# Cross-attention output by block of tokens for its last two column groups, and a hand-ordered second norm

## The chip, the cores and the metric

The kernel runs on one core of a Trainium2 chip. The metric is the time of one execution on the device in microseconds (us). Before the change it is 1125.58 us, the median of three runs (1125.52 to 1125.97).

The core's engines work side by side and each takes its instructions in order: TensorE (PE in the profile; PEld is its weight load), VectorE (DVE), ScalarE (ACT), GpSimd (POOL) and SyncE (SP), which issues the loads from memory.

## The reference

One layer of an encoder on 256 tokens of 2048 columns, all in float32. Around the change it does this:

```python
x  = layer_norm(ALPHA * x + mix, ln1_g, ln1_b)
xa = memory_cross_attention(x, mem_n, w_q_mem, w_kv_mem, w_o_mem)   # ends with o @ w_o_mem, 512 x 2048
x  = layer_norm(ALPHA * x + xa, ln2_g, ln2_b)
ff = square(relu(x @ w_mlp_in)) @ w_mlp_out                          # 2048 x 8192 and back
x  = layer_norm(ALPHA * x + ff, ln3_g, ln3_b)
```

`layer_norm` subtracts the mean over a token's 2048 columns, divides by the standard deviation, multiplies by a gain and adds a bias.

## The kernel before, in words

**Numbers as pairs.** TensorE multiplies a rounded form of float32. Every operand is therefore kept as two parts: hi, which is the value rounded, and lo, which is the value less hi. A product is the sum of three: hi times hi, hi times lo, lo times hi. `split` (L77) makes the pair: ACT writes hi (L79), DVE subtracts for lo (L80).

**Tokens and tiles.** The 256 tokens are two blocks of 128. `res[b]` holds the residual of block b, tokens on partitions, 2048 columns. For the next matrix product the activations must be transposed: `x2t` holds 16 row tiles k of 128 columns, each with 256 tokens of hi and 256 of lo.

**Weights.** A `Stream` (L115) loads a weight unit (128 x 2048, one megabyte) into one of three raw tiles through SP and splits it in two halves of 1024 columns into `w_hi` and `w_lo`, of which there are four buffers each. A half's buffer comes free when the products that read it are done. `next()` gives one half.

**The cross-attention output** (L677 to L685). Four column groups n of 512; each takes two halves of `w_om`. `proj_tokens` (L150) makes 4 row tiles x 2 blocks x 3 products of 512 columns, block after block within a row tile; for n = 3 it goes by block: all of block 0, then block 1 in two halves of 256 columns. After each group DVE adds the PSUM tile to the scaled residual (L683) and takes the statistics of that piece (L490).

**The second norm** (L689, `norm_transposed`, L501). `moments` gives mean and 1/deviation of a block: aggregate on DVE (L495), a small addition on DVE (L88), a power of -1/2 on POOL (L91). `scale(n)` subtracts the mean and multiplies, in place, on 512 columns of each block (L513, DVE). `turn(k)` treats two row tiles: four transposes on PE into one PSUM tile (L526; there are four such tiles), gain and bias into a temporary, the first row tile on ACT (L534), the second on DVE (L531), then one split of both row tiles into `x2t` (L79, L80). The norm is cut into pieces, scale 0, turn 0, scale 1, turn 2 and so on. Between them four halves of the first MLP weights are split (L692); four others already lie in `wide_0`.

**The first MLP products** (L721). `together` makes four column tiles at once, row tile by row tile: for each of 16 row tiles four pairs of a 512-column product (L193) and a 256-column product (L195; L192 for the last row tile). Two row tiles of `x2t` and one half of weights serve each step. Later column tiles take their weights from `s_in`.

**What sets the order.** A scheduler places each engine's instructions by a timing reckoning of its own and by priority in the order of the program. `pin` (L74) puts an instruction behind whatever the program had last for the same engine. Before the change only the splits of those four halves of MLP weights are pinned here; a hand-made edge keeps the later scalings behind the first.

Of the kernel before, what the change touches and what calls it, by code (L numbers as in the profile page):

```python
# [11 lines left out]
F32 = mybir.dt.float32  # L12
F32R = mybir.dt.float32r
BF16 = mybir.dt.bfloat16
AF = mybir.ActivationFunctionType
# [23 lines left out]
def encoder_kernel(ctx: ExitStack, tc: tile.TileContext, t, out):  # L39
# [56 lines left out]
    def pump(n=1):  # L96
        """Issues n of the pieces of work that run beside the products."""
        for _ in range(n):
            if side:
                side.popleft()()  # L100
# [4 lines left out]
    def busy(n):  # L105
        """Keeps the array's clock up while it waits."""
        ps = acc_tile()
        for _ in range(n):
            tc.keep_in_program_order(
                nc.tensor.matmul(ps, ones, ones[:, None, :].broadcast_to([P, 4, P]),  # L110
                                 start=True, stop=True))
# [3 lines left out]
    class Stream:  # L115
        """Halves of weight units, loaded and split in the order in which they are asked for."""

# [30 lines left out]

    # xt: [128, k, 512] holds the transposed activations, hi in 0:256, lo in 256:512.
    def proj_tokens(stream, xt, nk, cols, before=None, by_block=None, wide=None):  # L150
        """Tokens on partitions: two PSUM tiles [128, cols], one a block of tokens. By block,
        the second comes in two halves of the columns, each behind the one before."""
        ps = [acc_tile() for _ in range(NB + bool(by_block))]
# [29 lines left out]
    def cols_mm(ps, hi, lo, xt, k, nk):  # L183
        """Columns on partitions: PSUM [128, 256] += a [k, 128] tile of weights."""
        nc.tensor.matmul(ps, hi, xt[:, k, 0:S], start=k == 0, stop=False)  # L185
        nc.tensor.matmul(ps, hi, xt[:, k, S:2 * S], start=False, stop=False)  # L186
        nc.tensor.matmul(ps, lo, xt[:, k, 0:S], start=False, stop=k == nk - 1)  # L187

    def cols_mm_wide(ps, hi, lo, xt, k, nk):
        """The same into [128, 512]: the products with the activations' lo in 256:512."""  # L190
        if k == nk - 1:
            nc.tensor.matmul(ps[:, 0:S], lo, xt[:, k, 0:S], start=False, stop=False)  # L192
        nc.tensor.matmul(ps, hi, xt[:, k, :], start=k == 0, stop=k == nk - 1)  # L193
        if k < nk - 1:
            nc.tensor.matmul(ps[:, 0:S], lo, xt[:, k, 0:S], start=False, stop=False)  # L195

    def transpose_split(dst, src, k0, b, nk=4, width=P):
        """Transposes src [128 tokens, nk * 128] into dst[:, k0:k0+nk] at the block's place."""
        ps = att_tile()
        for j in range(nk):  # L200
            nc.tensor.transpose(ps[:, j * P:(j + 1) * P], src[:, j * P:(j + 1) * P], ident)
        o = b * P
        v = ps[:, :nk * P].rearrange("p (k c) -> p k c", c=P)
        split(dst[:, k0:k0 + nk, o:o + P], dst[:, k0:k0 + nk, S + o:S + o + P], v)

# [1 line left out]
    tab_a = resp.tile([P, D], F32, tag="res", name="tab_a")  # L207
# [7 lines left out]

# [1 line left out]
    xt_t = big.tile([P, KT * 512], F32R, tag="big", name="xt")  # L217
# [3 lines left out]
    def load_x(k):  # L221
        """The row tiles of x^T from k on."""
        n = 1 if k < 2 else 0 if k % 2 else 2
# [29 lines left out]

# [1 line left out]
    def latent(stream, g, dst):  # L255
# [11 lines left out]
    def qk_heads(ps, b, nh, tc_, ts_, dst, h0, sc=1.0):  # L267
        """RMS norm, gain and rotation of nh heads [128, nh * 128], then their transposes."""
        w = nh * DH
# [23 lines left out]

# [1 line left out]
    class Heads:  # L295
        """Heads of attention under way: the scores of one, the weights of the one before, the
        values of the one before that."""

# [15 lines left out]
    def softmax(terms, pt=None):  # L314
        """terms: (q [128, 512], k [128, 512]) pairs, hi | lo, summed into the scores.
        Returns the transposed weights of attention, hi | lo."""
        s = att_tile()
# [166 lines left out]

# [1 line left out]
    def stats_tile():  # L486
        return [small.tile([P, 5, 6], F32, tag="bn", name="bn"), 0]

    def stats(st, x):
        nc.vector.bn_stats(st[0][:, st[1], :], x)  # L490
        st[1] += 1

    def moments(st):
# [6 lines left out]

    def norm_transposed(x, sts, i, dst, vec=False, before=None):  # L501
        """x(b, n) <- (x(b, n) - mean) * rstd in place; dst <- its transpose with gain and bias, split.
        Returns the pieces of that work behind the moments."""
        mom = [moments(sts[b]) for b in range(NB)]

        ahead = []

        def scale(n):
            if before is not None:
                before(n)  # L510
            for b in range(NB):
                mu, r = mom[b]
                ins = nc.vector.tensor_scalar(out=x(b, n), in0=x(b, n), scalar1=mu, scalar2=r,  # L513
                                              op0=ALU.subtract, op1=ALU.mult)
                if n and ahead:
                    tc.add_manual_dep(ins.ins, ahead[0], mybir.DependencyInfo(
                        mybir.DependencyClass.NoSync, mybir.DependencyReason.DATA))
            if vec and not n:
                ahead.append(ins.ins.name)

        def turn(k, n=2):
            ps, y = att_tile(), tmp_tile()
            for j in range(n):
# [5 lines left out]
                g, c = gbt[:, i, 0, k + j:k + j + 1], gbt[:, i, 1, k + j:k + j + 1]  # L529
                if j == 1 and vec:  # L530
                    nc.vector.tensor_scalar(out=y[:, o], in0=ps[:, o], scalar1=g, scalar2=c,  # L531
                                            op0=ALU.mult, op1=ALU.add)
                else:
                    nc.scalar.activation(y[:, o], ps[:, o], AF.Identity, scale=g, bias=c)  # L534
            ins = split(dst[:, k:k + n, 0:S], dst[:, k:k + n, S:2 * S],
                        y[:, :n * S].rearrange("p (j c) -> p j c", j=n))

# [8 lines left out]
    def residual(name):  # L546
        """res <- res * gain + bias, as pieces."""
        rows = {}
# [22 lines left out]

# [1 line left out]
    sts = [stats_tile() for _ in range(NB)]  # L573
# [42 lines left out]

# [1 line left out]
    attC = big.tile([P, 8192], F32R, tag="big", name="attC")  # L618
# [4 lines left out]
    def together(nexts, xt_, mm, outs):  # L623
        """Several column tiles at once, k by k."""
        n = len(outs)
# [49 lines left out]
    pump(len(side))  # L675

    sts = [stats_tile() for _ in range(NB)]  # L677
    s_om = Stream(t["w_om"])
    for n in range(4):
        ps = proj_tokens(s_om, om, HM, 512, by_block=n == 3)  # L680
        for b, c, w, p_ in ps:
            r = res[b][:, n * 512 + c:n * 512 + c + w]
            nc.vector.scalar_tensor_tensor(out=r, in0=r, scalar=ALPHA, in1=p_[:, :w],  # L683
                                           op0=ALU.mult, op1=ALU.add)
            stats(sts[b], r)  # L685
    x2t = big3("x2t")
    s_mi0.pinned = True
    w_mi0 = [(wide_0[:, u, 0, :], wide_0[:, u, 1, :]) for u in range(4)]
    for i, piece in enumerate(norm_transposed(res_chunk, sts, 2, x2t, vec=True)):  # L689
        piece()  # L690
        if i in (5, 7, 9, 11):
            w_mi0.append(s_mi0.next())  # L692

# [1 line left out]
    s_in, s_mo = Stream(t["w_mi"]), Stream(t["w_mo"])  # L695
# [10 lines left out]
    def last_weights(k):  # L706
        """The last group's weights stay on chip whole, for one block of tokens after the other."""
        hi, lo = wide_w[0][:, k * 512:(k + 2) * 512], wide_w[1][:, k * 512:(k + 2) * 512]
# [65 lines left out]
def _rows(w, kt, cols):  # L774
    """[K, N] -> units [n * kgroups, 128, kt * cols]: kt row tiles of one group of columns."""
    k, n = w.shape
# [4 lines left out]
def _pairs(w, d):  # L781
    """Rotation pairs of each d columns side by side -> firsts, then seconds."""
    s = w.shape[:-1]
# [102 lines left out]
```

## Time and profile before

| | |
|---|---|
| median of the runs | 1125.58 us |
| profiled execution, span from first to last instruction | 1123.8 us |
| TensorE busy | 1108.1 us, 99% |
| DVE busy | 740.9 us, 66% |
| ACT busy | 541.4 us, 48% |
| last product of the cross-attention output ends | 393.97 us |
| first MLP product starts | 402.16 us |

Times within the execution are microseconds from the start of the span. A row of a time line gives start, duration, engine, line, operation, what is written from what, and how many instructions are merged in it; in brackets stands how long the engine sat idle before it and what ended that. A row of busy times by stretch gives the stretch, then the busy time of PE, PEld, DVE, ACT and POOL (with the number of instructions), then the granted share of TensorE's clock, the share of the DMA engines, and GB/s. A row of the chain of waits gives start, duration and what. Matmuls are pipelined: a product recorded with 0.39 us starts 0.23 us after the one before.

### The profile page before, as it was taken

What the parts mean: (1) busy time and instruction counts of PE and PEld (TensorE: products, weight loads), DVE (VectorE), ACT (ScalarE), POOL (GpSimd) and SP (SyncE); (2) the same over time, 40 slices, a digit from 0 to 9 for tenths busy, and PEclk for the clock granted to TensorE, in tenths of its full rate; (3) what the DMA queues carried; (4) which work ended last, traced back from release to release, by engine and by line L of the source; (5) the groups of instructions that cost most, each with busy time, mean ns of one, the idle gap of its engine ahead of it and who ended that gap; (6) DMA issues with size and microseconds to landing.
All of it is one profiled execution on the core that took longest, in us unless ns stands there. A gap on an engine that the chain in (4) does not pass through costs nothing.

```text
span 1123.8 us, 14990 instructions
## 1 busy us (share of the span) xinstructions
PE 1108.1 (99%) x6004; PEld 955.1 (85%) x6004; DVE 740.9 (66%) x1036; ACT 541.4 (48%) x778; POOL 38.2 (3%) x45
## 2 busy tenths in 40 slices
PE   9999999999999999999999999999999999999996
PEld 6988899888998878888888888888888888888885
DVE  5878677688798778855556664556665546665575
ACT  6555665546576355443345443344444334444440
POOL 1402000000100000000000000000000000000000
PEclk9999999999999999999999999999999999999998
DMA  9664454476466426655555555555555555555572
GB/s 336 223 225 151 150 187 150 152 241 243 161 225 252 150 75 225 226 187 187 187 190 189 185 186 192 201 199 188 184 186 198 188 188 187 188 187 187 190 260 76
DMA packets 37942, 215.85 MB, mean 192 GB/s; under 512 B 4336, under 2 KB 5232, under 8 KB 14192
## 3 DMA queue, kind: packets, MB, share of 16 engines
q1 hardware_dynamic: 37872, 214.89, 54.4%
q8 instruction: 47, 0.77, 0.3%
q14 instruction: 23, 0.19, 0.0%
HBM read 212.78 MB, written 2.10 MB: 191 GB/s over the span
## 4 chain that ended last, share of the span: by engine, by line
PE 96%; DMA 2%; DVE 1%; ACT 0%; issue 0%; SPq 0%; POOL 0%; DVEq 0%; ACTq 0%
PE acc L193 21%; PE acc L147 17%; PE acc L145 17%; PE acc L146 17%; PE acc L195 10%; PE acc L187 2%; PE acc L186 2%; PE acc L185 2%; PE att L526 1%; DMA raw<-in_w_qa 1%; PE att L341 1%; DMA raw<-in_w_ka 1%; PE acc L192 1%; PE att L147 1%; PE att L146 1%; PE att L145 1%
## 5 line engine op out<-in xcount | busy, mean ns | idle before, releaser
L80 DVE TENSOR_TENSOR w_lo<-raw,w_hi 128x1024 fp32r<-128x1024 f32 (+2 forms) x374 | 445.0, 1193 | 272.5 <-ACT w_hi L79 267.8
L79 ACT ACTIVATE w_hi<-raw 128x1024 fp32r<-128x1024 f32 (+2 forms) x374 | 385.8, 1034 | 372.4 <-PE acc L147 259.0
L193 PE MATMUL acc<-x2t,w_hi 128*128 128x512 f32 x992 | 346.4, 399 | 0.0
L195 PE MATMUL acc<-x2t,w_lo 128*128 128x256 f32 x928 | 261.0, 281 | 0.0
L193 PEld LDWEIGHTS acc<-x2t,w_hi 128*128 128x128 f32 x992 | 182.8, 188 | 40.4 <-DVE tmp L702 0.2
L147 PE MATMUL acc<-w_hi,ht 128*128 128x512 f32 x480 | 187.0, 389 | 0.0
L146 PE MATMUL acc<-w_lo,ht 128*128 128x512 f32 x480 | 186.9, 389 | 0.0
L145 PE MATMUL acc<-w_hi,ht 128*128 128x512 f32 x480 | 186.8, 390 | 0.0
L195 PEld LDWEIGHTS acc<-x2t,w_lo 128*128 128x128 f32 x928 | 175.7, 189 | 2.8
L146 PEld LDWEIGHTS acc<-w_lo,ht 128*128 128x128 f32 x480 | 90.2, 188 | 18.8
L147 PEld LDWEIGHTS acc<-w_hi,ht 128*128 128x128 f32 x480 | 90.2, 188 | 18.8
L145 PEld LDWEIGHTS acc<-w_hi,ht 128*128 128x128 f32 x480 | 90.1, 188 | 18.2
L701 ACT ACTIVATE tmp<-acc 128x256 f32<-128x256 f32 x64 | 24.4, 383 | 110.0 <-PE acc L193 110.0
L146 PE MATMUL acc<-w_lo,xt 128*128 128x512 f32 (+2 forms) x192 | 69.4, 362 | 0.5 <-DVE w_lo L80 0.5
L147 PE MATMUL acc<-w_hi,xt 128*128 128x512 f32 (+2 forms) x192 | 69.2, 362 | 0.0
L145 PE MATMUL acc<-w_hi,xt 128*128 128x512 f32 (+2 forms) x192 | 65.6, 361 | 1.1 <-ACT w_hi L79 1.1
L702 DVE TENSOR_TENSOR tmp<-acc,tmp 128x256 f32<-128x256 f32 x64 | 27.1, 425 | 54.2 <-ACT tmp L701 54.2
L147 PE MATMUL acc<-w_hi,ot 128*128 128x512 f32 (+1 forms) x136 | 52.0, 382 | 0.0
L146 PE MATMUL acc<-w_lo,ot 128*128 128x512 f32 (+1 forms) x136 | 51.7, 380 | 0.0
L145 PE MATMUL acc<-w_hi,ot 128*128 128x512 f32 (+1 forms) x136 | 51.2, 380 | 0.0
L91 POOL TENSOR_TENSOR rs_r<-rs_v,mhalf 128x1 f32<-128x1 f32 (+2 forms) x18 | 17.1, 952 | 944.1 <-DVE rs_v L88 944.0
L145 PEld LDWEIGHTS acc<-w_hi,xt 128*128 128x128 f32 x192 | 35.7, 189 | 6.9 <-ACT w_hi L79 2.4
(209 smaller groups left out, 1406.8 us busy)
## 6 DMA issues: line engine op xcount, KB each, us to landing
raw<-in_w_mi SPq DMA_DIRECT2D x64, 1024.0 KB, 4.8
raw<-in_w_mo SPq DMA_DIRECT2D x64, 1024.0 KB, 4.8
raw<-in_w_out SPq DMA_DIRECT2D x16, 1024.0 KB, 5.0
raw<-in_w_b SPq DMA_DIRECT2D x5, 1024.0 KB, 4.8
raw<-in_w_qa SPq DMA_DIRECT2D x16, 256.0 KB, 5.4
raw<-in_w_qa SPq DMA_DIRECT2D x4, 1024.0 KB, 4.9
raw<-in_w_ckv SPq DMA_DIRECT2D x4, 1024.0 KB, 5.6
raw<-in_w_cq SPq DMA_DIRECT2D x4, 1024.0 KB, 4.7
```

The costliest lines, as they stand in the source:

```text
L79: pin(nc.scalar.activation(hi, src, AF.Copy), pinned)
L80: return pin(nc.vector.tensor_tensor(out=lo, in0=src, in1=f(hi), op=ALU.subtract), pinned)
L145: nc.tensor.matmul(ps, ah, bh, start=start, stop=False)
L146: nc.tensor.matmul(ps, ah, bl, start=False, stop=False)
L147: nc.tensor.matmul(ps, al, bh, start=False, stop=stop)
L185: nc.tensor.matmul(ps, hi, xt[:, k, 0:S], start=k == 0, stop=False)
L186: nc.tensor.matmul(ps, hi, xt[:, k, S:2 * S], start=False, stop=False)
L187: nc.tensor.matmul(ps, lo, xt[:, k, 0:S], start=False, stop=k == nk - 1)
L193: nc.tensor.matmul(ps, hi, xt[:, k, :], start=k == 0, stop=k == nk - 1)
L195: nc.tensor.matmul(ps[:, 0:S], lo, xt[:, k, 0:S], start=False, stop=False)
L701: nc.scalar.activation(lo, ps[:, S:2 * S], AF.Copy)
L702: nc.vector.tensor_tensor(out=h, in0=ps[:, 0:S], in1=lo, op=ALU.add)
```

## The change

Column groups 0 and 1 of the cross-attention output stay as they were. All four weight halves of groups 2 and 3 are then taken at once, and their products are made for block 0 first (both groups), then for block 1: group 2, and group 3 in two halves of 256 columns. The second norm is written out in one order, with every instruction of it pinned on its engine; block 0's statistics and three of its four scalings are put between block 1's products. For the first four row tiles (pairs p = 0 and 1) the gain on ACT writes the rounded hi part straight from PSUM into `x2t`, a gain on DVE writes the unrounded value, and DVE subtracts, one row tile at a time. The other pairs are converted as before. The same four halves of MLP weights are split between them, now behind pairs 3, 4, 5 and 6. The first norm, which shared `norm_transposed`, keeps its work; comments are dropped throughout.

```diff
-    for n in range(4):
-        ps = proj_tokens(s_om, om, HM, 512, by_block=n == 3)
-        for b, c, w, p_ in ps:
-            r = res[b][:, n * 512 + c:n * 512 + c + w]
-            nc.vector.scalar_tensor_tensor(out=r, in0=r, scalar=ALPHA, in1=p_[:, :w],
-                                           op0=ALU.mult, op1=ALU.add)
-            stats(sts[b], r)
+    def add_cross(b, c, w, p_, pinned=False):
+        r = res[b][:, c:c + w]
+        pin(nc.vector.scalar_tensor_tensor(out=r, in0=r, scalar=ALPHA, in1=p_[:, :w],
+                                           op0=ALU.mult, op1=ALU.add), pinned)
+        pin(stats(sts[b], r), pinned)
+    for n in range(2):
+        ps = proj_tokens(s_om, om, HM, 512)
+        for b in range(NB):
+            add_cross(b, n * 512, 512, ps[b])
+    om_w = [[s_om.next() for _ in range(2)] for _ in range(2)]
+    def cross_mm(b, n, c, w):
+        ps, o = acc_tile(), b * P
+        for k in range(HM):
+            hi, lo = (x[:, (k % 2) * 512 + c:(k % 2) * 512 + c + w] for x in om_w[n - 2][k // 2])
+            ah, al = om[:, k, o:o + P], om[:, k, S + o:S + o + P]
+            for i, (x, y) in enumerate(((ah, hi), (ah, lo), (al, hi))):
+                pin(nc.tensor.matmul(ps[:, :w], x, y, start=k == 0 and i == 0,
+                                     stop=k == HM - 1 and i == 2), True)
+        return ps
...
+    def turn2(b, p):
+        if p not in pst:
+            pst[p] = att_tile()
+        for j in range(2):
+            k, o = 2 * p + j, j * S + b * P
+            pin(nc.tensor.transpose(pst[p][:, o:o + P], res[b][:, k * P:(k + 1) * P], ident), True)
...
+    def convert(p):
+        ps, y = pst[p], tmp_tile()
+        if p < 2:
+            for j in range(2):
+                k, o = 2 * p + j, slice(j * S, (j + 1) * S)
+                gain2(x2t[:, k, 0:S], ps[:, o], k, True)
+                gain2(y[:, o], ps[:, o], k, False)
+                pin(nc.vector.tensor_tensor(out=x2t[:, k, S:2 * S], in0=y[:, o],
+                                            in1=f(x2t[:, k, 0:S]), op=ALU.subtract), True)
+        else:
+            for j in range(2):
+                gain2(y[:, j * S:(j + 1) * S], ps[:, j * S:(j + 1) * S], 2 * p + j, j == 0)
+            k = 2 * p
+            split(x2t[:, k:k + 2, 0:S], x2t[:, k:k + 2, S:2 * S],
+                  y.rearrange("p (j c) -> p j c", j=2), pinned=True)
+    for n in (2, 3):
+        add_cross(0, n * 512, 512, cross_mm(0, n, 0, 512), True)
+    mom[0] = moments_pinned(sts[0])
+    add_cross(1, 1024, 512, cross_mm(1, 2, 0, 512), True)
+    scale2(0, 0)
+    scale2(0, 1)
+    add_cross(1, 1536, 256, cross_mm(1, 3, 0, 256), True)
+    scale2(0, 2)
+    add_cross(1, 1792, 256, cross_mm(1, 3, 256, 256), True)
+    mom[1] = moments_pinned(sts[1])
+    for p in range(4):
+        turn2(0, p)
+    scale2(1, 0)
+    for p in range(2):
+        turn2(1, p)
+        convert(p)
+    scale2(1, 1)
+    for p in range(2, 4):
+        turn2(1, p)
+        convert(p)
     s_mi0.pinned = True
     w_mi0 = [(wide_0[:, u, 0, :], wide_0[:, u, 1, :]) for u in range(4)]
-    for i, piece in enumerate(norm_transposed(res_chunk, sts, 2, x2t, vec=True)):
-        piece()
-        if i in (5, 7, 9, 11):
+    scale2(0, 3)
+    w_mi0.append(s_mi0.next())
+    scale2(1, 2)
+    for p in range(4, 8):
+        if p == 6:
+            scale2(1, 3)
+        for b in range(NB):
+            turn2(b, p)
+        convert(p)
+        if p < 7:
             w_mi0.append(s_mi0.next())
```

`scale2(b, n)` is the scaling of one block's 512 columns, `moments_pinned` the moments of one block, `gain2` a gain on ACT or on DVE; each pins its instructions. Pair p of this diff is row tiles 2p and 2p + 1.

More of the change, by code (lines that the diff above doesn't have):

```diff
@@ L489, in stats @@
     def stats(st, x):
-        nc.vector.bn_stats(st[0][:, st[1], :], x)
         st[1] += 1
+        return nc.vector.bn_stats(st[0][:, st[1] - 1, :], x)
     def moments(st):
@@ L499, in res_chunk, with norm_transposed @@
         return res[b][:, n * 512:(n + 1) * 512]
-    def norm_transposed(x, sts, i, dst, vec=False, before=None):
+    def norm_transposed(x, sts, i, dst, before=None):
         mom = [moments(sts[b]) for b in range(NB)]
-        ahead = []
         def scale(n):
@@ L512, in scale @@
                 mu, r = mom[b]
[L513 to L519, printed above, removed]
+                nc.vector.tensor_scalar(out=x(b, n), in0=x(b, n), scalar1=mu, scalar2=r,
+                                        op0=ALU.subtract, op1=ALU.mult)
         def turn(k, n=2):
@@ L529, in turn @@
                 g, c = gbt[:, i, 0, k + j:k + j + 1], gbt[:, i, 1, k + j:k + j + 1]
-                if j == 1 and vec:
-                    nc.vector.tensor_scalar(out=y[:, o], in0=ps[:, o], scalar1=g, scalar2=c,
-                                            op0=ALU.mult, op1=ALU.add)
[L533 to L536, printed above, removed]
+                nc.scalar.activation(y[:, o], ps[:, o], AF.Identity, scale=g, bias=c)
+            split(dst[:, k:k + n, 0:S], dst[:, k:k + n, S:2 * S],
+                  y[:, :n * S].rearrange("p (j c) -> p j c", j=n))
         pieces = [lambda: scale(0)]
@@ L678, in encoder_kernel @@
     s_om = Stream(t["w_om"])
-    for n in range(4):
-        ps = proj_tokens(s_om, om, HM, 512, by_block=n == 3)
-        for b, c, w, p_ in ps:
-            r = res[b][:, n * 512 + c:n * 512 + c + w]
-            nc.vector.scalar_tensor_tensor(out=r, in0=r, scalar=ALPHA, in1=p_[:, :w],
-                                           op0=ALU.mult, op1=ALU.add)
-            stats(sts[b], r)
-    x2t = big3("x2t")
+    def add_cross(b, c, w, p_, pinned=False):
[3 more added lines that the diff above has]
+        pin(stats(sts[b], r), pinned)
@@ new lines, in moments_pinned @@
+    def moments_pinned(st):
+        mv = small.tile([P, 2], F32, tag="mv", name="mv")
+        pin(nc.vector.bn_aggr(mv, st[0][:, :st[1], :]), True)
+        v = small.tile([P, 8], F32, tag="rs_v", name="rs_v")
+        pin(nc.vector.tensor_scalar(out=v[:, :1], in0=mv[:, 1:2], scalar1=1.0, scalar2=LN_EPS,
+                                    op0=ALU.mult, op1=ALU.add), True)
+        r = small.tile([P, 8], F32, tag="rs_r", name="rs_r")
+        pin(nc.gpsimd.tensor_tensor(out=r[:, :1], in0=v[:, :1], in1=mhalf[:, :1], op=ALU.pow), True)
+        return mv[:, 0:1], r[:, :1]
@@ new lines, in encoder_kernel, with scale2 @@
+    mom = [None, None]
+    def scale2(b, n):
+        x, (mu, r) = res_chunk(b, n), mom[b]
+        pin(nc.vector.tensor_scalar(out=x, in0=x, scalar1=mu, scalar2=r,
+                                    op0=ALU.subtract, op1=ALU.mult), True)
+    x2t = big3("x2t")
+    pst = {}
+    def turn2(b, p):
[4 more added lines that the diff above has]
+            pin(nc.tensor.transpose(pst[p][:, o:o + P], res[b][:, k * P:(k + 1) * P], ident), True)
@@ new lines, in gain2 @@
+    def gain2(y, ps, k, act):
+        g, c = gbt[:, 2, 0, k:k + 1], gbt[:, 2, 1, k:k + 1]
+        if act:
+            pin(nc.scalar.activation(y, ps, AF.Identity, scale=g, bias=c), True)
+        else:
+            pin(nc.vector.tensor_scalar(out=y, in0=ps, scalar1=g, scalar2=c,
+                                        op0=ALU.mult, op1=ALU.add), True)
+    def convert(p):
[7 more added lines that the diff above has]
+                                            in1=f(x2t[:, k, 0:S]), op=ALU.subtract), True)
+        else:
+            for j in range(2):
[3 more added lines that the diff above has]
+                  y.rearrange("p (j c) -> p j c", j=2), pinned=True)
```

## The prediction

> **What bounds the kernel now.** I read the page first, then the busy time by stretches around the change, then the chain of waits, then the time lines of the single engines.
>
> ```profile
> span 1123.8 us, 14990 instructions
> PE 1108.1 (99%) x6004; PEld 955.1 (85%) x6004; DVE 740.9 (66%) x1036; ACT 541.4 (48%) x778; POOL 38.2 (3%) x45
> ```
>
> TensorE (PE) is busy for all but 1%, so time can be won only where it idles or runs throttled. The profiled span is 1123.8 us and the median of the runs is 1125.58, so 1.8 us lie around the span; I take them as unchanged and add my difference to the median. About 0.2% (2.25 us) is what a measurement of this kernel can tell from no change.
>
> ```profile
> 393.97:402.16 8.19, 5.56 (x28) 3.78 (x27) 7.50 (x20) 4.01 (x8) 1.08 (x2) 0.79 0.00 0
> 402.16:425.10 22.94, 22.94 (x136) 20.17 (x134) 14.86 (x20) 12.00 (x19) 0.00 (x0) 1.00 0.33 119
> ```
>
> By stretches (PE, weight load, DVE, ACT, POOL, granted clock): between the last product of the cross-attention output (393.97) and the first MLP product (402.16) PE is busy for 5.56 of 8.19 us, all transposes, while DVE is busy 7.50. From 402.16 on PE never stops. So the stage is a serial stretch of 8.2 us, and then 22.9 us of products. The chain of waits says what holds the first product:
>
> ```profile
> 389.27 0.23 PE acc L146
> 392.18 0.12 PE acc L145
> 394.09 0.34 DVE res L683
> 394.50 0.41 DVE bn L490
> 394.93 0.29 DVE mv L495
> 395.70 0.07 DVE rs_v L88
> 395.84 0.55 POOL rs_r L91
> 396.41 0.56 DVE res L513
> 397.02 0.44 PE att L526 x2
> ```
>
> Add and statistics of block 1 (L683, L490, L495), the power on POOL (L91), the scaling (L513), then transposes. The transposes are not the real holder; DVE is:
>
> ```profile
> 396.41 3.28 DVE L513 TENSOR_SCALAR res<-res,mv,rs_r 128x512 f32<-128x512 f32 x7 [0.66 <-POOL rs_r L91]
> 399.62 1.89 DVE L531 TENSOR_SCALAR tmp<-att,gbt 128x256 f32<-128x256 f32 x4
> 401.43 1.28 DVE L80 TENSOR_TENSOR x2t<-tmp,x2t 128x512 fp32r<-128x512 f32 x2
> 402.16 0.50 PE L193 MATMUL acc<-x2t,wide 128*128 128x512 f32 x1
> ```
>
> Seven scalings stand ahead of the first gain on DVE, and the first product follows the first lo half. Durations by shape (busy, mean ns of one):
>
> ```profile
> L80 DVE TENSOR_TENSOR w_lo<-raw,w_hi 128x1024 fp32r<-128x1024 f32 x12 | 14.6, 1221 | 13.0 <-ACT w_hi L79 13.0
> L80 DVE TENSOR_TENSOR x2t<-tmp,x2t 128x512 fp32r<-128x512 f32 x8 | 5.3, 682 | 0.2 <-ACT x2t L79 0.2
> L79 ACT ACTIVATE x2t<-tmp 128x512 fp32r<-128x512 f32 x8 | 4.8, 622 | 2.5 <-DVE tmp L531 2.5
> L683 DVE SCALAR_TENSOR_TENSOR res<-res,acc 128x512 f32<-128x512 f32 x7 | 4.6, 683 | 1.7 <-PE acc L147 1.7
> L490 DVE BATCH_NORM_STATS2 bn<-res 128x6 f32<-128x512 f32 x7 | 4.5, 682 | 0.0
> L534 ACT ACTIVATE tmp<-att,gbt 128x256 f32<-128x256 f32 x8 | 4.1, 557 | 13.4 <-PE att L526 13.4
> L531 DVE TENSOR_SCALAR tmp<-att,gbt 128x256 f32<-128x256 f32 x8 | 4.0, 535 | 0.1
> ```
>
> The first lo half ends at 401.43 + 0.68 = 402.11, and the product starts 0.05 later: I use 0.05 for every hand-over. Two lo halves in a row take 1.28 and not 1.36, so on DVE the next independent instruction starts 0.08 before an end.
>
> **The change, part by part.** *Products.* Column groups 2 and 3 keep their products (36 of 512 columns at 0.23, 24 of 256 at 0.12); they only go block by block, so PE's end stays at 393.97 if the weights are there. Block 0 of group 3 now starts 24x0.12 + 12x0.23 + 12x0.23 = 8.4 us ahead of that end, at 385.6, and needs the second half of its weights 1.4 us later, at 387.0.
>
> ```profile
> 385.15 1.22 DVE L80 TENSOR_TENSOR w_lo<-raw,w_hi 128x1024 fp32r<-128x1024 f32 x1
> 391.86 1.14 DVE L683 SCALAR_TENSOR_TENSOR res<-res,acc 128x512 f32<-128x512 f32 x2 [1.57 <-PE acc L147]
> ```
>
> That half is split by 386.4: cover of 0.6 us, cost nothing; without it, each us late would be one us of PE. Block 0's moments and three of its scalings now lie under block 1's products, as DVE's 1.57 us of idle there shows room.
>
> *Start of the conversions.* On DVE, behind block 1's group 2 (PSUM complete at 391.1): add and statistics of 512 columns 2x0.68, two scalings at 3.28/7 = 0.47, add and statistics of the first 256 columns (0.43 each, 394.50 to 394.93), one scaling 0.47. That is 3.6 us and reaches 394.7, against 394.0 when the last products land. Then add and statistics 0.9, aggregate 0.3, and, as the chain has it, 0.2 to POOL and 0.57 there and back with DVE's own start, 0.8 in all, to the scaling: 396.7 (396.0 if DVE were free at once; before: 396.41). So the moments do not come sooner. The gain lies behind them: one scaling (0.56) and the two transposes instead of seven scalings and four gains. Rows for the rest:
>
> ```profile
> 397.38 2.08 ACT L534 ACTIVATE tmp<-att,gbt 128x256 f32<-128x256 f32 x4 [13.36 <-PE att L526]
> 371.73 1.42 DVE L80 TENSOR_TENSOR attC<-att,attC 128x256 fp32r<-128x256 f32 x4 [0.39 <-ACT attC L79]
> 416.90 1.06 ACT L79 ACTIVATE w_hi<-raw 128x1024 fp32r<-128x1024 f32 x1 [4.92 <-PE acc L193]
> 418.00 1.23 DVE L80 TENSOR_TENSOR w_lo<-raw,w_hi 128x1024 fp32r<-128x1024 f32 x1 [4.40 <-ACT w_hi L79]
> ```
>
> Scaling to transpose 0.61, transpose to gain 0.36 (397.02 to 397.38), gain to x2t 0.6, difference of 256 columns about 0.42 (four take 1.42: 0.36 each in a row and the overlap once): first product at 396.7 + 0.61 + 0.36 + 0.6 + 0.42 + 0.05 = 398.7, 3.4 us before 402.16.
>
> *What PE must still do.* Ten to twelve transposes run before the first product, twenty among the products; before, six did. Their price:
>
> ```profile
> 406.77 0.40 PE L193 MATMUL acc<-x2t,wide 128*128 128x512 f32 x1
> 407.12 0.38 PE L526 MATMUL att<-ident,res 128*128 128x128 f32 x2
> 407.69 0.39 PE L193 MATMUL acc<-x2t,wide 128*128 128x512 f32 x1
> 409.19 0.40 PE L193 MATMUL acc<-x2t,wide 128*128 128x512 f32 x1
> 423.41 0.39 PE L193 MATMUL acc<-x2t,w_hi 128*128 128x512 f32 x1
> 424.92 0.39 PE L193 MATMUL acc<-x2t,w_hi 128*128 128x512 f32 x1
> ```
>
> 41 pairs of products (L193 and L195) from 409.19 to 423.41 are 0.347 us a pair; two pairs with two transposes (406.77 to 407.69) took 0.92 instead of 0.69, so 0.115 a transpose. If PE were never kept waiting: 398.7 + 64x0.347 + 20x0.115 = 423.2, against 424.92 + 0.23 = 425.15 before. That is the most the change can win: 1.95 us.
>
> *The fixed order as a chain.* But each conversion is now pinned behind the one before on ACT and on DVE, and so are the splits of the last four halves of MLP weights (w_hi on ACT, w_lo on DVE) between them. Summed from rows:
> - pairs 0 and 1 of row tiles, after the first gain starts (397.7): gain 0.58 and difference 0.36 for each of four tiles: 3.8, so block 1's second scaling starts at 401.5.
> - to the gain of pair 2: 0.61 + 0.5 (second transpose); then gain to hi 0.57, hi to lo 0.66, lo to next gain 0.6; pair 3 again 0.57 + 0.66 + 0.6; block 0's last scaling 0.47; w_lo 1.14; block 1's third scaling starts at 407.9.
> - 1.1 to pair 4's gain (409.0). From there each pair is a closed loop: gain to hi 0.57, hi to w_hi 0.55, w_hi to w_lo 1.1 (416.90 to 418.00), w_lo to the next gain 1.15: 3.37 us. Three loops and block 1's last scaling with its transposes (1.1) bring pair 7's gain to 420.2; hi 0.57, lo 0.68 after another 0.66 end it at 422.1. A transpose that is ready waits for the products ahead of it in PE's queue, 0 to 0.35 at each of two places of this chain; I take 0.2 in all: 422.3.
> - hand-over and pair 7's products, 0.05 + 8x0.347 = 2.8: **425.2**.
>
> PE takes 8x0.347 + 4x0.115 = 3.23 us for a pair, the loop 3.37 plus 1.1 once, so PE eats up its lead and then waits, about 2 us in all, for pairs 5 to 7. The 3.4 us won at the start are paid back: 14x0.115 = 1.6 in transposes that are no longer ahead of the products, 2 in these waits. 425.2 against 425.15 is 0.1 us slower: 1125.7. Bounds of the unknown terms: the moments between 396.0 and 396.7 (0.7 us towards faster); a price of 0.36 to 0.42 for the differences (0.1); the waiting transposes between 0 and 0.7 (0.5 towards slower).
>
> SP's queue stays. The last raw tile of weights is freed by the last split, at about 420, and SP's load of the third unit of the next weights waits for that; this unit is first used two column tiles (2x16x0.347 = 11 us) after 425, and a load takes 4.8 us by the page's list of DMA issues:
>
> ```profile
> raw<-in_w_mi SPq DMA_DIRECT2D x64, 1024.0 KB, 4.8
> ```
>
> So that costs nothing.
>
> **The rivals.**
>
> *A. PE remains the bound* (the chain runs 2 us shorter than my sum, for instance because ACT and DVE hand over faster or the moments come at 396.0). For it: the products before ran without a stop behind the same number of splits. Against it: there the last lo half was late by nothing only because the scheduler could put splits and gains where they fitted. It would give 423.2, so 1123.6. The clock belongs to this rival:
>
> ```profile
> 396.40:397.60 1.20, 0.57 (x3) 0.33 (x4) 1.19 (x3) 0.22 (x1) 0.00 (x0) 1.00 0.00 0
> 398.80:400.00 1.20, 1.20 (x8) 1.11 (x6) 1.20 (x3) 0.66 (x2) 0.00 (x0) 0.50 0.00 0
> 401.10:402.16 1.06, 1.05 (x9) 0.61 (x7) 1.06 (x3) 1.06 (x3) 0.00 (x0) 1.00 0.00 0
> ```
>
> After the idle stretch the granted clock fell to 0.50 between 397.6 and 401.1, about 3.4 us, when only transposes ran. In the changed kernel the same idle stretch stands ahead of products: at half clock 3.4 us lose 1.7 us of them, which leaves 1125.3 where PE is the bound, and nothing where the chain is (its 2 us of waits absorb it). [...] Since the row shows the drop once, at one place of the idle stretch, I give A with a fast clock 0.12 (1123.6) and A with the slow one 0.10 (1125.3).
>
> *B. Splits of the next weights enter the chain.* L79's row at 416.90 waited for PE to free a buffer; with products starting earlier those buffers come free from row tile 9 on (398.7 + 40x0.347 + 14x0.115 = 414.2), while the pinned chain still runs, and these splits are not pinned. A w_lo (1.14) in DVE's gap of 0.64 ahead of pair 6's gain (1.1 less the scaling's 0.47) costs 0.5; the next half's w_hi (1.06), put on ACT into the 0.15 or so ahead of pair 6's hi, 0.9; its w_lo, only partly on the way of the last loop, an estimated 0.2: 1.6 us, 1127.3. It decides if the scheduler thinks the buffer free before pair 6's hi.
>
> *C. Transposes too early in PE's queue.* The transposes are pinned to each other, the products are put between them by the scheduler's own reckoning. If pair 6's transposes stand ahead of the products of row tile 8, these wait for block 1's last scaling (416.2): 416.7 + 32x0.347 + 4x0.115 = 428.3, 3.1 us slower, 1128.8. It decides if fewer than ten of the sixteen row tiles stand ahead of them: with ten it is 425.5. Against it: the six transposes among the products before cost only their 0.115 each, never a wait.
>
> **How the numbers follow.** My forecast (the chain eats the gain) 0.50, A 0.12 and 0.10, B 0.16, C 0.12. The time is that of the forecast, 1125.7. The range leaves out C and a little of the far side of A: 1123.5 to 1127.8. Faster by over 0.2% (under 1123.3) needs A with the moments at 396.0 and no slow clock: 0.06. Slower by over 0.2% is C and the case of B together with late transposes: 0.15. The rest, 0.79, is within 0.2%.
>
> **What would show it.** Right: first product near 398.7 instead of 402.16; twenty transposes among the products; PE idle about 2 us before the row tiles of pairs 5, 6 and 7, ended by DVE's x2t; the last of the first four column tiles at about 425. The start is wrong if block 1's scaling comes before 396 or after 397; the chain is wrong if PE shows no waits behind 399 (A), if w_hi or w_lo of later weights stand between pairs 5 and 7 (B), or if transposes wait for a scaling while converted tiles lie ready (C). A change over 2.3 us either way would prove the sum of the chain wrong.

## The result, and the profile after

| | before | after |
|---|---|---|
| median of the runs | 1125.78 us | 1138.02 us (1137.63 to 1139.98) |
| ratio to before, 95% interval | | 1.0111 [1.0098, 1.0123] |
| profiled execution, span | 1123.8 us | 1135.9 us |
| last product of the cross-attention output ends | 393.97 us | 393.70 us |
| first MLP product starts | 402.16 us | 399.38 us |
| last product of the first four column tiles ends | 425.15 us | 437.39 us |

The change is 12.2 us slower, 10.2 us above the top of the predicted range. The start came out nearly as forecast, 2.8 us earlier than before. The 64 pairs of products behind it then take 38.0 us instead of 23.0. The page, and busy times by stretch (PE, PEld, DVE, ACT, POOL, granted clock):

```profile
span 1135.9 us, 14984 instructions
PE 1113.5 (98%) x6004; PEld 960.4 (85%) x6004; DVE 744.7 (66%) x1040; ACT 542.4 (48%) x778; POOL 35.7 (3%) x45
```

```profile
393.90:399.30 5.40, 1.49 (x12) 1.02 (x10) 3.41 (x9) 1.06 (x3) 0.54 (x1) 0.98 0.00 0
399.30:402.50 3.20, 3.12 (x10) 2.67 (x10) 2.82 (x7) 1.09 (x3) 0.00 (x0) 0.50 0.00 0
402.50:406.20 3.70, 3.70 (x23) 3.24 (x22) 0.46 (x1) 0.00 (x0) 0.00 (x0) 1.00 0.02 4
406.20:409.30 3.10, 1.26 (x10) 0.95 (x9) 1.44 (x3) 1.65 (x3) 0.00 (x0) 1.00 0.00 0
409.30:412.70 3.40, 3.40 (x11) 2.92 (x12) 2.71 (x5) 1.58 (x2) 0.00 (x0) 0.50 0.00 0
...
416.40:419.50 3.10, 1.13 (x11) 0.89 (x9) 1.24 (x2) 2.03 (x3) 0.00 (x0) 1.00 0.00 0
419.50:423.00 3.50, 3.50 (x11) 3.02 (x12) 2.41 (x4) 2.14 (x4) 0.00 (x0) 0.51 0.35 56
...
426.70:429.80 3.10, 0.91 (x9) 0.68 (x7) 1.24 (x2) 2.10 (x4) 0.00 (x0) 1.00 0.00 0
429.80:433.20 3.40, 3.40 (x11) 2.92 (x12) 3.33 (x4) 2.90 (x5) 0.00 (x0) 0.50 0.29 58
```

Read it as one cycle that comes back: PE at half clock for 3.4 us (four times), PE at full clock while ACT and DVE do next to nothing (402.50 to 406.20: ACT 0.00, DVE 0.46), then PE nearly idle while ACT and DVE work (three times). The engines take turns. PE's waits in this stretch, who was late and for how long (total, times, longest):

```profile
PE acc L193 <- DVE x2t L80: 6.2, 4, 2.2
PE att L719 <- DVE res L707: 2.4, 1, 2.4
PE acc L193 <- ACT x2t L724: 1.6, 1, 1.6
```

The time lines show why. First DVE's scalings of block 1 (L707) and the splits ahead of the last pair, then PE's transposes (L719) and the products that waited:

```profile
402.42 0.54 DVE L707 TENSOR_SCALAR res<-res,mv,rs_r 128x512 f32<-128x512 f32 x1
...
412.45 0.54 DVE L707 TENSOR_SCALAR res<-res,mv,rs_r 128x512 f32<-128x512 f32 x1
...
424.11 0.54 DVE L707 TENSOR_SCALAR res<-res,mv,rs_r 128x512 f32<-128x512 f32 x1
...
431.47 2.35 DVE L80 TENSOR_TENSOR w_lo<-raw,w_hi 128x1024 fp32r<-128x1024 f32 x2
433.74 0.69 DVE L80 TENSOR_TENSOR x2t<-tmp,x2t 128x512 fp32r<-128x512 f32 x1
```

```profile
406.15 0.82 PE L719 MATMUL att<-ident,res 128*128 128x128 f32 x6
...
409.15 0.68 PE L193 MATMUL acc<-x2t,wide 128*128 128x512 f32 x1 [1.84 <-DVE x2t L80]
...
416.44 1.03 PE L719 MATMUL att<-ident,res 128*128 128x128 f32 x8
419.44 0.72 PE L193 MATMUL acc<-x2t,w_hi 128*128 128x512 f32 x1 [1.97 <-DVE x2t L80]
...
426.67 0.82 PE L719 MATMUL att<-ident,res 128*128 128x128 f32 x6
429.67 0.71 PE L193 MATMUL acc<-x2t,w_hi 128*128 128x512 f32 x1 [2.19 <-DVE x2t L80]
...
434.47 0.50 PE L193 MATMUL acc<-x2t,w_hi 128*128 128x512 f32 x1 [0.19 <-DVE x2t L80]
```

Each scaling is done long before its transposes run: 402.96 against 406.15, 412.99 against 416.44, 424.65 against 426.67. In between PE works off all products of the row tiles that are already converted. Only when these are used up, but for one pair of products at the first place, do the next six or eight transposes come, and then nothing is left on PE to cover the conversion. Its length is read from the chain of waits:

```profile
396.55 0.56 DVE res L707
397.15 0.45 PE att L719 x2
397.63 0.57 ACT x2t L724
398.23 0.56 DVE tmp L726
398.81 0.57 ACT x2t L724
399.38 0.76 PE acc L193
...
406.57 0.57 ACT tmp L724
407.17 0.55 DVE tmp L726
407.75 0.64 ACT x2t L79
408.41 0.70 DVE x2t L80
409.15 0.68 PE acc L193
```

Gain on ACT, gain on DVE, hi, lo: four steps in a row, 2.6 us from 406.57 to 409.15. The two gains of a pair write different halves but read the same PSUM tile, and DVE's begins only after ACT's (which ends at 407.14; DVE's starts at 407.17).

The loss adds up as follows. The start is 2.8 us earlier. PE idles 6.2 us among the products (38.01 us less 31.83 busy). At half clock a pair of products starts every 0.64 us (409.85, 410.49, 411.13) instead of every 0.347, so 46% of such a stretch is lost: of 3.1 us of products in the first and 3.4 in each of the three others, 6.1 us together. Fourteen more transposes stand among the products, 1.6 by the prediction's 0.115. That is 11.1 of the 12.1 us by which the spans differ; the last 1.0 I don't assign.

### The profile page after: what moved, and what is told of

The parts are those of the page before. It is cut to its first block, busy times and chain, and to the rows that moved or that the text cites. A ratio compares the mean times of both kernels' runs of the same rounds, so it can differ in the third digit from the quotient of the medians.

```text
span 1135.9 us, 14984 instructions
## 1 busy us (share of the span) xinstructions
PE 1113.5 (98%) x6004; PEld 960.4 (85%) x6004; DVE 744.7 (66%) x1040; ACT 542.4 (48%) x778; POOL 35.7 (3%) x45
## 4 chain that ended last, share of the span: by engine, by line
PE 97%; DVE 1%; ACT 1%; DMA 0%; issue 0%; POOL 0%; DVEq 0%; SPq 0%
PE acc L193 22%; PE acc L145 18%; PE acc L146 17%; PE acc L147 17%; PE acc L195 10%; PE acc L187 2%; PE acc L185 2%; PE acc L186 2%; PE att L341 1%; PE acc L689 1%; PE acc L192 1%; PE att L519 1%; PE att L146 1%; PE att L147 1%; PE att L145 1%; PE att L353 0%
```

## The experiments

Four theories had to be told apart. **Q**: the places of the transposes in PE's queue cost the time, since conversions start too late. **G**: the half clock after each idle stretch does. **S**: the conversion is too long, because the gains of a pair run one after the other on a pinned chain. **B**: splits of the next weights enter that chain. Medians of the same kernel (before) differed by up to 0.4 us between the groups of runs, so smaller differences are not read.

**by_block_alone.** The projection by block of tokens as in the change, the norm as before:

```diff
     add_cross(1, 1792, 256, cross_mm(1, 3, 256, 256), True)
-    mom[1] = moments_pinned(sts[1])
...
+    for i, piece in enumerate(norm_transposed(res_chunk, sts, 2, x2t, vec=True)):
+        piece()
+        if i in (5, 7, 9, 11):
+            w_mi0.append(s_mi0.next())
```

> Only the column groups by block of tokens; the second norm is that of before. Theory Q (in PE's queue the transposes stand behind products, 3.2, 3.4 and 2.0 us after their scalings are done, and PE then idles until they are converted), theory G (the half clock after each idle stretch is most of the loss) and theory S (the pinned chain of ACT and DVE, in which the two gains of a pair wait for each other on one PSUM tile, binds wherever the transposes stand) all put the loss into the norm: 1124 to 1126 us. The rival, that the order by block itself costs (weights late, block 1's moments late), says 1129 or more.

Measured: 1125.60 us, ratio 1.0001 [0.9992, 1.0010]. Its busy times by stretch look like those of before, with one stretch at half clock among the transposes and then products without a stop:

```profile
396.40:399.80 3.40, 2.94 (x14) 2.56 (x14) 3.40 (x8) 1.94 (x4) 0.00 (x0) 0.50 0.00 0
...
402.00:425.00 23.00, 23.00 (x134) 20.01 (x133) 14.62 (x19) 11.70 (x18) 0.00 (x0) 1.00 0.32 115
```

The block order costs nothing and, with the old norm, brings nothing. The whole loss lies in the rewritten norm: its order, its pins and its conversions.

**turns_not_pinned.** The change with its transposes left to the scheduler:

```diff
-            pin(nc.tensor.transpose(pst[p][:, o:o + P], res[b][:, k * P:(k + 1) * P], ident), True)
+            nc.tensor.transpose(pst[p][:, o:o + P], res[b][:, k * P:(k + 1) * P], ident)
```

> The changed kernel, its transposes alone not pinned; the scheduler then puts them behind 4, 12 and 14 pairs of products and again behind 32 and 48 (8 and 4 of them). Q: the first long wait goes, two stay, about 1134. S: nothing changes, 1138. G: one stretch of half clock less, 1.6 us, 1136.4.

Measured: 1136.73 us, ratio 1.0097 [1.0082, 1.0112]. PE still waits four times, 6.7 us in all:

```profile
PE acc L193 <- DVE x2t L80: 6.7, 4, 2.4
```

So the pins on the transposes are not what places most of them late. With them free, the scheduler splits the first group (two, two and four transposes, at 402.82, 405.91 and 406.71) but keeps a group of eight and one of four behind whole row tiles of products. The time is G's 1136.4 and not Q's 1134: the first long wait did not go, it fell from 1.84 to 1.58 us. The 1.3 us that the run gains is about one stretch at half clock: this run has three of them. Its second idle stretch, 1.58 us long, was followed by none:

```profile
405.90:409.80 3.90, 2.32 (x17) 1.83 (x15) 1.37 (x3) 1.65 (x3) 0.00 (x0) 1.00 0.00 0
409.80:413.20 3.40, 3.40 (x20) 2.96 (x21) 2.70 (x5) 1.58 (x2) 0.00 (x0) 1.00 0.00 0
```

**products_by_hand.** The change with the first MLP products pinned too, and the transposes put between them by hand, most of them one or two row tiles earlier. ACT's and DVE's order stays:

```diff
+    prod(0, 1, 2)
+    turn2(1, 2)
+    turn2(1, 3)
+    prod(3)
+    convert(2)
+    convert(3)
...
+    prod(4, 5)
+    turn2(1, 4)
+    convert(4)
+    prod(6)
+    turn2(0, 5)
...
```

> The changed kernel with the first MLP products pinned too, and the transposes of pairs 2 to 7 put between them at the places where their scalings are done; ACT and DVE keep their order. Q: the chain of ACT and DVE then ends at about 427.9 instead of 437, 1128.5, up to 1131 if stretches of half clock remain. S: the chain binds as before, 1135 or more. G alone: no wait is long enough to lower the clock but the first, 1131 to 1132.

Measured: 1132.32 us, ratio 1.0056 [1.0039, 1.0073], 5.7 us less than the change, but short of the 1128.5 to 1131 that Q would give, and close to the 1131 to 1132 of G alone. The clock is halved for two stretches on end (398.3 to 405.1; the first 24 products take 6.3 us, 400.66 to 406.96, and not 12x0.347 = 4.2) where the change has four, which by 1.6 us a stretch is about 3 of the 5.7. So this run alone does not tell Q from G. The longest wait behind the first product stands ahead of the last pair:

```profile
430.06 0.49 PE L766 MATMUL acc<-x2t,w_hi 128*128 128x512 f32 x1 [1.72 <-DVE x2t L80]
```

There two unpinned splits of the next weights (2.35 us on DVE) had gone ahead of pair 7's lo half, as in the change at 431.47. That is B, at work once Q is partly mended.

**dummies_in_waits.** The change's own order on PE, written down and pinned, with 46 products of a tile of ones put where PE idled; their PSUM tile is read by nobody:

```diff
+    warm(dum, 10)
     scale2(1, 0)
...
+    warm(dum, 6)
...
+    warm(pst[4], 10)
...
```

> The changed kernel's own order on PE, pinned, with products of ones that nothing reads put into the idle stretches (10 and 6 before the first product, 10 in each of the three later waits), so that PE stays busy while it waits. G: all four stretches of half clock (6 us by their pairs at 0.64 instead of 0.347 us) go, 1132, and what stays over 1125.6 is waiting. If the half clock lies beside the waits and costs nothing: 1138. If the clock were the whole of it: 1126.

Measured: 1137.14 us, ratio 1.0101 [1.0086, 1.0116]: a miss. The clock stayed full up to 432, yet nearly nothing was won. The reason is in DVE's and PE's time lines:

```profile
426.05 3.50 DVE L80 TENSOR_TENSOR w_lo<-raw,w_hi 128x1024 fp32r<-128x1024 f32 x3 [0.26 <-ACT w_hi L79]
...
431.05 0.69 DVE L80 TENSOR_TENSOR x2t<-tmp,x2t 128x512 fp32r<-128x512 f32 x1
```

```profile
431.79 0.50 PE L773 MATMUL acc<-x2t,w_hi 128*128 128x512 f32 x1 [2.90 <-DVE x2t L80]
```

The first of the three splits in that row is the pinned one behind pair 6. The two others, and one more at 429.92 (1.22 us), are unpinned splits of the next weights; they stand ahead of pair 7's gain and of its lo half. PE waits 2.90 us for that half, and behind the wait the clock is halved (432.2 to 435.6). I had expected G to show undisturbed and had left B out.

**dummies_splits_behind.** The same, with the first two splits of the next weights pinned behind pair 7's conversion:

```diff
     prod(12, 13, 14, 15)
+    s_in = Stream(t["w_mi"])
+    s_in.pinned = True
+    in_w = [s_in.next() for _ in range(2)]
+    s_in.pinned = False
```

> The dummies in the waits again, with the next weights' first two splits pinned behind pair 7's conversion. G with B (the splits took back what the clock gave: a wait of 2.9 us ahead of row tile 14): 1137.1 - 2.9 - 1.3 (the last half clock goes too) = 1132.9. If the splits were not the cause of that wait: 1137.

Measured: 1133.72 us, ratio 1.0068 [1.0055, 1.0082], against 1132.9 expected; the clock is full throughout. So clock and splits together are 1138.0 - 1133.7 = 4.3 us of the loss, and about 8 us over before remain in the order, now covered by the dummies instead of shown as idle time (1.0 of them is a wait for DVE ahead of the next column tile, which comes with the splits moved back). The dummies themselves delay nothing: behind them the products start 0.05 to 0.06 us after the lo half that they need (408.03 against 407.97, 416.68 against 416.63, 425.90 against 425.84). And the transposes still come late at full clock: 405.02, 413.68 and 422.89, against scalings done at 402.98, 411.87 and 421.90.

**by_hand_splits_behind.** products_by_hand with the same two splits pinned behind pair 7.

> The products by hand, and the first two splits of the next weights pinned behind pair 7's conversion, on ACT and on DVE. Theory Q with B (two such splits stood ahead of pair 7's conversion and made the last wait of 1.7 us): 1132.3 - 1.7 = 1130.6. If they only filled gaps: 1132.3, no change.

Measured: 1132.27 us, ratio 1.0056 [1.0042, 1.0069]: no change against products_by_hand, where 1.7 us less was expected. The wait ahead of pair 7 fell from 1.72 to 0.24 us, but the splits that were moved back now hold DVE (3.50 us for three splits, from 427.26) when the results of the first column tiles are to be taken, and the next products wait for that:

```profile
PE acc L193 <- DVE tmp L818: 1.0, 1, 1.0
```

**by_hand_clock_held.** The last kernel with dummies ahead of its first product, so that the clock is full as in dummies_splits_behind; the two then differ only in where transposes and products stand on PE:

```diff
+    warm(dum, 10)
     scale2(1, 0)
...
+    warm(dum, 6)
     prod(0, 1, 2)
```

> by_hand_splits_behind (132.27 over 1000, so 1132.27 us) with products of ones, read by nobody, between the transposes ahead of the first product, so that the clock is not halved there; the transposes' places, the conversions and the splits stay. It stands against dummies_splits_behind (1133.7): clock full in both, splits behind in both, only the places of transposes and products in TensorE's queue differ. Theory Q (transposes behind products cost time even at a full clock): half a clock for 3.4 us loses 1.6 us in by_hand_splits_behind, so 1130.6, and 3 us under dummies_splits_behind. Theory G alone (the order of the queue costs only by way of the clock): as dummies_splits_behind, 1133.7. If the clock's loss is covered by the conversions that the products wait for anyway, it stays at 1132.3.

Measured: 1129.91 us, ratio 1.0038 [1.0024, 1.0051]. Against dummies_splits_behind that is 3.8 us for the order alone, at a full clock in both: Q is shown without G. Against by_hand_splits_behind it is 2.4 us for the clock by the medians, against 1.6 expected; the spans of the two profiled executions, of which the first has one stretch at half clock (400.3 to 403.7; its first 24 products take 5.8 us, in the second 4.2), differ by 1.7 (1129.8 and 1128.1).

**by_hand_gains_on_act.** by_hand_splits_behind with both gains of pairs 2 to 7 on ACT:

```diff
-                gain2(y[:, j * S:(j + 1) * S], ps[:, j * S:(j + 1) * S], 2 * p + j, j == 0)
+                gain2(y[:, j * S:(j + 1) * S], ps[:, j * S:(j + 1) * S], 2 * p + j, True)
```

> The run before, and for pairs 2 to 7 both gains on ACT, so that DVE's gain no longer waits for ACT's on the same PSUM tile. S: six pairs lose up to 0.6 us each where the chain of ACT and DVE is what PE waits for (four of them): 1130.6 - 1.7 = 1128.9. If the waits of PE come from the order alone, 1130.6.

Measured: 1129.64 us, ratio 1.0035 [1.0021, 1.0049], 2.6 us less than by_hand_splits_behind. ACT's time line:

```profile
412.27 1.02 ACT L724 ACTIVATE tmp<-att,gbt 128x256 f32<-128x256 f32 x2 [2.36 <-PE att L719]
413.32 0.63 ACT L79 ACTIVATE x2t<-tmp 128x512 fp32r<-128x512 f32 x1
```

Two gains on one engine take 1.02 us, and hi begins 1.05 us after the first gain did. Shared between two engines that was 1.18 in the change (406.57 to 407.75), for they don't overlap and pay two hand-overs of 0.03 each (407.14 to 407.17, 407.72 to 407.75). That is 0.13 us a pair, at most 0.8 in six pairs: the gains still run one after the other, so this alone is the small part. The larger part shows in DVE's order. In by_hand_splits_behind DVE's next gain comes only behind a w_lo split, and hi waits for that gain:

```profile
413.40 0.55 DVE L726 TENSOR_SCALAR tmp<-att,gbt 128x256 f32<-128x256 f32 x1 [1.13 <-ACT tmp L724]
414.64 0.69 DVE L80 TENSOR_TENSOR x2t<-tmp,x2t 128x512 fp32r<-128x512 f32 x1 [0.70 <-ACT x2t L79]
415.59 1.23 DVE L80 TENSOR_TENSOR w_lo<-raw,w_hi 128x1024 fp32r<-128x1024 f32 x1 [0.26 <-ACT w_hi L79]
416.74 0.54 DVE L726 TENSOR_SCALAR tmp<-att,gbt 128x256 f32<-128x256 f32 x1
```

From pair 4's gain to pair 5's it is 3.34 us there. With the gains on ACT it is 2.54 (412.27 to 414.81), because ACT makes the next gains (414.81 to 415.81) while DVE splits (the w_hi that its split needs ends at 414.91); the same holds from pair 6 to pair 7. Two such loops are 1.6 of the 2.6 us, though how much of that PE felt is not taken apart. So S holds as a chain of ACT and DVE that is too long, while the shared PSUM tile is the smaller part of it.

**order_mended.** All of it together: block 1's first two scalings right behind its moments, all sixteen transposes of the first four pairs ahead of the first product, the others one or two pairs ahead of their conversion, all gains on ACT, 12 dummies ahead of the first product, the two splits behind pair 7:

```diff
     mom[1] = moments_pinned(sts[1])
+    scale2(0, 2)
...
+    warm(dum, 8)
     scale2(1, 0)
...
+    warm(dum, 4)
     scale2(1, 1)
...
+    scale2(0, 3)
+    convert(0)
...
+    prod(0, 1)
+    convert(1)
+    for b in range(NB):
+        turn2(b, 4)
+    prod(2, 3)
...
```

> The changed kernel with block 1's scalings right behind its moments, gains on ACT alone (pair 0 row tile by row tile), transposes of each pair on PE one pair or two ahead of its products, all pinned, dummy products in the two waits ahead of the first product, and the next weights' splits behind pair 7. Q, S and B together: first product 5.0 us after the last cross-attention product, 64 pairs at 0.347, 16 transposes among them at 0.115: 29.1 us, against 31.3 before: 1123.3. If the order by block or the direct conversion were at fault themselves, 1127 or more.

Measured: 1123.87 us (1123.40 to 1124.26, 11 runs), ratio 0.9982 [0.9973, 0.9991]: 0.18% faster than the kernel before, and 14 us faster than the change. PE's time line has the twelve dummies and eight of the first sixteen transposes ahead of the first product. Behind it the other transposes stand in groups of four well ahead of need, and PE idles nowhere:

```profile
395.04 1.89 PE L758 MATMUL acc<-ones 128*128 128x512 bf16 x8
397.39 1.11 PE L719 MATMUL att<-ident,res 128*128 128x128 f32 x8 [0.46 <-DVE res L707]
398.34 1.03 PE L758 MATMUL acc<-ones 128*128 128x512 bf16 x4
399.39 2.97 PE L772 MATMUL acc<-x2t,wide 128*128 128x512 f32 x15
```

```profile
399.39:422.60 23.21, 23.21 (x138) 20.46 (x139) 13.99 (x17) 18.15 (x29) 0.00 (x0) 1.00 0.30 100
```

**Three parts of it taken back.** mended_no_dummies leaves the dummies out. mended_hi_straight converts pairs 0 and 1 as the change does it. mended_old_block_order makes the projection as before, by block only for the last column group; block 0's scalings move back with it.

```diff
-    warm(dum, 8)
-    warm(dum, 4)
```

```diff
-        if p < 1:
+        if p < 2:
...
-                gain2(y[:, o], ps[:, o], k, True)
-                pin(nc.scalar.activation(x2t[:, k, 0:S], y[:, o], AF.Copy), True)
+                gain2(x2t[:, k, 0:S], ps[:, o], k, True)
+                gain2(y[:, o], ps[:, o], k, False)
```

```diff
-    for n in range(2):
+    for n in range(3):
...
-    for n in (2, 3):
-        add_cross(0, n * 512, 512, cross_mm(0, n, 0, 512), True)
+    add_cross(0, 1536, 512, cross_mm(0, 3, 0, 512), True)
...
-    add_cross(1, 1024, 512, cross_mm(1, 2, 0, 512), True)
```

> order_mended (1123.87 us) without its 12 products of ones ahead of the first product. Theory G: the idle stretch before the first product halves the clock once, for 3.4 us in which products run, 1.4 to 1.6 us: 1125.4. If the conversions of the first row tiles are the bound there, or the window falls on transposes alone as in the kernel before: 1123.9.

> order_mended (1123.87 us) with the first four row tiles converted as the change does it: ACT writes the rounded hi part straight from PSUM, DVE the unrounded value from the same PSUM tile, then the difference. Theory S: DVE's gain waits for ACT's on the same PSUM tile, 0.6 us a pair of gains, and in exchange the second pass of ACT is saved: 0.2 to 0.6 us later, 1124.1 to 1124.5. If the straight hi part were at fault for the change's loss: 1126 or more. If straight hi saves what it was meant to save: 1123.3.

> order_mended (1123.87 us) with the output projection as in the kernel before (only the last column group by block of tokens), the rest of the order kept. Block 0's scalings then come later, behind the last products, two of them on the way to block 1's moments or to its transposes: about 1 us later, 1124.9. If the block order of group 2 is worth nothing even in the mended order, as it was in by_block_alone: 1123.9.

Measured: 1125.57 us without dummies (0.9998 [0.9989, 1.0006]), 1124.17 with hi straight from PSUM (0.9990 [0.9981, 0.9999]), 1125.06 with the old block order (0.9995 [0.9986, 1.0004]). The dummies are worth 1.7 us by the medians. Without them the mended order is no faster than the kernel before, and the clock is halved for two stretches, while products run; in the kernel before it was one, on transposes alone (397.6 to 401.1):

```profile
397.70:404.60 6.90, 6.10 (x21) 5.33 (x21) 3.86 (x8) 6.73 (x13) 0.00 (x0) 0.51 0.01 2
```

The block order is worth 1.2 us here by the medians, and nothing in by_block_alone. The two intervals overlap a little, but the traces agree: without it the first product starts at 400.54 instead of 399.39. It pays only when the norm behind it can use the earlier statistics. Hi straight from PSUM costs 0.3 us by the medians, which these intervals don't tell from nothing; in any case it isn't what cost the 12 us. Its two gains are again one behind the other on DVE's time line:

```profile
398.26 0.54 DVE L726 TENSOR_SCALAR tmp<-att,gbt 128x256 f32<-128x256 f32 x1 [0.22 <-ACT x2t L724]
```

## Why the prediction was wrong

**The step that failed** is the one on PE's queue: "a transpose that is ready waits for the products ahead of it in PE's queue, 0 to 0.35 at each of two places", 0.2 us in all. The trace has 3.2, 3.45 and 2.0 us at three places. The end of the chain, pair 7's lo half, was forecast at 422.1 and came at 434.4; those 8.65 us are the largest part of the 12.3 between them. I had let the transposes slip between the products wherever their scaling was done, since the kernel before did so. But PE kept the order in which the scheduler had placed its instructions (transposes whose scaling was done at 402.96 ran at 406.15, behind products), and only half of that order was written in the diff: transposes follow each other, products follow each other, and where the one goes between the other the scheduler decided by its own reckoning. I looked at that and priced it in rival C, with the direction reversed: transposes too early, so that products wait behind them, 3.1 us. They came too late, and behind them a whole conversion lay bare. The experiments bear it out: 3.8 us lay between two orders at a full clock in both, and 5.7 us came back when transposes and products were put in order by hand, some 3 of them through the clock. The lateness feeds on the clock, since the products ahead of the transposes run at half clock; at full clock it is still 2.0, 1.8 and 1.0 us (dummies_splits_behind). Unpinning the transposes brought only 1.3 us, so the diff's pins on them aren't the main cause. Why the scheduler's reckoning put the products first is not shown by any run.

**The clock.** The prediction took one stretch at half clock, "nothing where the chain is", because idle time would absorb it. There were four, one for each idle stretch, and products ran in each. Holding the clock brought 4.3 us at the change's own order, together with moving the splits back; alone it brought 2.4 at the order by hand and 1.7 at the mended one.

**The two gains of a pair.** The sum had them side by side. They ran one behind the other, 0.60 us more (406.57 to 407.17) wherever a conversion begins anew behind transposes: at pairs 0, 2, 4 and 6. The first product, forecast at 398.7, came at 399.38, and this step is 0.6 of the 0.7 us between them. The loop of gain, hi, w_hi and w_lo, sized 3.37 us, was right as it was pinned: DVE's gain of pair 5 starts 3.33 us after that of pair 4 (417.46 to 420.79), since ACT's gain there lies under DVE's split. What was avoidable in it is seen in by_hand_gains_on_act. The rows show that DVE's gain is released by ACT's on the same PSUM tile, and that no two gains on one tile overlap in the change; on two different tiles they did (DVE's gain for pair 0 from 399.41, under ACT's for pair 1, which ends at 399.83). What orders them on one tile no run shows. I had not weighed that wait.

**What held.** The block order was free, as forecast (by_block_alone). Block 1's scaling came at 396.55 against 396.7. The price of transposes held where PE is the bound: in order_mended 64 pairs and 16 transposes make 64x0.347 + 16x0.115 = 24.05 us, and the time line has 24.4 (399.39 to the start of the last product at 423.56 plus 0.23). Rival A's bound, a win of at most 1.95 us, was about reached by order_mended with 1.7 to 2.1, in another order and with dummies. Rival B happened one pair later than described: two splits of the next weights stood between pair 7's gain and its lo half (431.47). In the change that ended only a wait of 0.19 us; it cost once the other waits were filled (dummies_in_waits 1137.14 us, with the splits moved back 1133.72). The forecast that the pinned chain just eats the gain assumed a chain on ACT and DVE that starts a pair while PE still has products; the late transposes took that overlap away.

## What to carry to other kernels

When one engine's instructions are pinned and those between them are not, the order that comes out is unknown until it is looked at: write both streams down in one order, or count on the worst place. Bring what starts a long chain on other engines (here a transpose of 0.1 us that releases 2.6 us of conversion) as early in the queue as its inputs allow, and keep at least one such chain's length of work behind it. Idle time of TensorE can cost more than its length: here the clock was halved for 3.4 us behind waits of 1.84 us and more among the products.

## What the runs showed of the hardware

- The stretches at half clock last 3.4 us and begin 10.2 us apart in the change (399.1, 409.3, 419.6, 429.8), three times their length, and they don't follow the products: the one that ends the idle time starts 0.3 us behind the first beginning and 0.1 to 0.2 us ahead of the other three. What sets these times no run shows.
- Among the products, idle stretches of 1.84, 1.97 and 2.19 us were followed by half clock, as were 2.40 and 2.41 in turns_not_pinned and 2.90 in dummies_in_waits; those of 1.58 (turns_not_pinned) and up to 1.72 us (products_by_hand) were not.
- Products of ones that nobody reads, 0.23 us each, held the clock: with 12 of them (order_mended) it was 1.00 from 399.39 on, without them (mended_no_dummies) 0.51 for 6.9 us, and they were worth 1.7 us, because PE sat idle there without them (2.2 us in one wait, against 0.5).
